# Seven products for the second up-projection pair, its block sums made during the attention

## The chip, the cores and the metric

The kernel runs on one core of a Trainium2 chip. TensorE does the matrix products, VectorE and ScalarE the elementwise work, GpSimd (POOL) a few scalings and the issue of accumulating transfers, SyncE the issue of the other transfers. The metric is device time in microseconds (us) of one execution. Every time below is in us unless ns is written.

## The reference

One layer of a decoder: forgetting attention, a residual with layer norm, a gated MLP with a causal depthwise convolution, another residual with layer norm, and a gated embedding. 512 rows, width 1024, all in float32. The part that the change touches is the MLP's first product:

```python
def conv_ffn(x, w_up, conv_w, conv_b, w_down):
    u, g = jnp.split(x @ w_up, [FFN_DIM], axis=-1)      # x 512 x 1024, w_up 1024 x 5632
    g = causal_dwconv(g, conv_w, conv_b)                # three taps along the rows
    return (jax.nn.gelu(g, approximate=False) * u) @ w_down   # w_down 2816 x 1024
...
x = layer_norm(ALPHA * x + fox_mixer(x, ...), ...)
x = layer_norm(ALPHA * x + conv_ffn(x, ...), ...)
gate = sigmoid(x @ ple_w_gate + ple_b_gate)
x = x + gate * (p @ ple_w_proj)
```

## The kernel before

**Numbers in two parts.** Each float32 operand is split into a high part (rounded to the matmul's format) and a low part, and each product is three matmuls: high x high, high x low, low x high (`three`, its matmul is L159). A weight piece is cut in two steps: ScalarE copies it to `whi` (L130), VectorE subtracts to make `wlo` (L136). With `by_dma` the low part is made in another way: ScalarE writes the negated high part into `wlo` (L132), and POOL issues a transfer that adds the weight onto it from DRAM (L133).

**The weight stream.** The class `Weights` holds a list of pieces ("units") of 128 x 1024 float32 in the order of use. `load_to` loads them into four raw buffers; some pieces instead go to a part of a tile called `side`, chosen by `spare` (`W.more`), so that more loads are in flight. `cut_to` cuts them, into five `whi` and five `wlo` buffers. `get(i, 4)` cuts up to piece i+4 before the product on piece i is emitted. Some pieces carry a `make`: VectorE adds or subtracts blocks before the cut (`t12` L215 and L216, `up_t3` L229, `t4` L237).

**The up-projection in pairs.** The 22 column blocks of `w_up` (f) are taken as pairs j = f // 2, numbered from 0, so j = 1 is the second pair. A plain pair is four pieces (u and g of two blocks), each with 8 x 3 matmuls of 512 rows' columns, in `up`. The pairs in `UP_PAIRS` are computed by a Strassen-like scheme with seven half-size products instead of eight (`up_step`): stages 0, 1 and 2 have one piece for g (s = 0) and one for u (s = 1), with 24 matmuls of 256 columns each; stage 3 has one piece for both. After stage 0 ScalarE copies half of the bank away (`side(7)`, L913) and zeroes that half (L914), and VectorE adds the other half to the copy (L918); after stage 1 ScalarE copies both halves out (L922, L923, L925); after stage 2 VectorE subtracts the whole bank (L929); after stage 3 ScalarE copies (L933). The scheme needs sums of the input's blocks (`x_sums`, made once) and sums of weight blocks. Those weight sums come from one of three places:

- pairs in `KEPT`: VectorE makes them during the attention (`keep_load`, `keep_sums`), and they are kept in DRAM;
- pairs in `IN_DRAM`: a copy of the blocks is made in DRAM (`up_copies`, issued at heads in `COPIES`), then accumulating transfers add blocks in DRAM (`sums_beside`, one step at each place in `BESIDE`);
- the others: the `make` functions on the spot.

Each step of `sums_beside` is a one-column ScalarE copy (L320), a one-column POOL copy behind it (L321), and a POOL transfer (L322). After the pairs it also sums blocks of the gate weight.

**The rest of a pair.** The convolution is a ScalarE pass (L855) and two VectorE passes (L856, L858), then Gelu on ScalarE (L863) and the product on VectorE (L864). For pairs in `APART` the sums of the previous pair's result (`operand_sums`, L951 to L954) and its split (`operand_parts`, L959 and L960) are made in this pair's stage 0. The second weight's products (`down`) follow one group of three pairs later, a few between the stages of the pairs from j = 3 on (`between`, `CHUNKS`); pairs 0 to 2 have none between their stages.

**Order.** A planner orders the instructions by estimated times. From the second pair to the end of the MLP's pairs, VectorE and ScalarE are held to the order of the program:

```python
if f == 2:
    ordered.enter_context(tc.manual_schedule(
        engines={mybir.EngineType.DVE, mybir.EngineType.Activation}))
```

After the pairs comes a remainder of the second product (`r`), four times `norm`, then the embedding and the gate (again with block sums, loaded as `gt`).

Of the kernel before, what the change touches and what calls it, by code (L numbers as in the profile page):

```python
# [12 lines left out]
AF = mybir.ActivationFunctionType  # L13
# [3 lines left out]
P = 128  # L17
# [13 lines left out]

CHUNKS = (None,) + ((1,) * 8 + (0, 1, 2, 1),) * 2 + ((1, 1, 2, 1, 2, 2, 2, 1),)

UP_PAIRS = (2, 3, 4, 5, 6, 7, 8, 9)

KEPT = (3, 4, 5, 6, 7)

IN_DRAM = (8,)

BESIDE = {2: (0, 2, 3), 3: (0, 2, 3), 4: (0, 2, 3), 5: (0, 2), 6: (0, 2, 3), 7: (0, 2), 8: (0, 2, 3),  # L40
          9: (0, 2, 3), 10: (0, 2)}

DMA_PAIRS = (1, 2)

APART = (2, 3, 4, 5, 6, 7, 8, 9)
HALF = S // 2
ALPHA = 2.0 ** 0.25
EPS = 1e-5
# [9 lines left out]
RAW_BUFS = 4  # L58

COPIES = (2, 3)  # L60

BANKS = ("six", "six", "two", "six", "six", "six", "two", "six")
SPLIT_BUFS = 5
# [86 lines left out]
def trunk_layer(ctx: ExitStack, tc: tile.TileContext, xT, x2d, pT, w0, wqk, wv1, wv2, bf, wo, wup, cwb,  # L150
                wdn, wpl, wg, bg, gm, bm, gf, bff, out):
    nc = tc.nc
# [21 lines left out]
    W = Weights(tc, base)  # L174
# [78 lines left out]
    def up_units(j):  # L253

        f0, f1 = 2 * j, 2 * j + 1
        if j in KEPT + IN_DRAM:
            return (lambda q: W.add(wup[f0, 1 - q], inner=P),
                    lambda q: W.add(kept[j, q][:, 0:4:3, :], inner=512),
                    lambda q: W.add([(kept[j, q][:, 2, :], 512), (wup[f1, 1 - q][:, 4:], 512)]),
                    lambda q: W.add([(kept[j, i][:, 1, :], 512) for i in range(2)]))  # L260

        def unit(f, q, make=None):
            return W.add(wup[f, 1 - q], inner=P, make=make, by_dma=make is None and j in DMA_PAIRS)

        add = nc.vector.tensor_add
        return (lambda q: unit(f0, q), lambda q: unit(f1, q, t12(wup[f0, 1 - q][:, :4], 3 + q, add)),
                lambda q: unit(f1, q, up_t3),
                lambda q: W.add([(wup[f0, 1 - i][:, 4:], 512) for i in range(2)], make=t4(3, op=add)))

    dram = ctx.enter_context(tc.tile_pool(name="dram", bufs=1, space=bass.MemoryType.DRAM))  # L270
    kept = {(j, q): dram.tile([P, 4, 512], F32, name=f"kept{j}_{q}")
            for j in KEPT + IN_DRAM for q in range(2)}

# [18 lines left out]
    def up_copies():  # L292

        for j in IN_DRAM:
            for q in range(2):
                for n in range(2):
                    nc.sync.dma_start(kept[j, q][:, 2 * n:2 * n + 2, :].rearrange("p a (k b) -> p (a k) b", b=P),
                                      wup[2 * j + n, 1 - q])
                    yield

    def sums_beside():

        def blocks(j):
            for to, src in ((0, None), (2, None), (3, 0), (1, 3)):
                for q in range(2):
                    t = kept[j, q]
                    if src is None:
                        yield (t[:, to, :].rearrange("p (k b) -> p k b", b=P),
                               wup[2 * j + 1, 1 - q][:, 2 * to:2 * to + 4])
                    else:  # L310
                        yield t[:, to, :], t[:, src, :]

        def gates():
            for to, src in (("t1", "b12"), ("t2", "t1"), ("t4", "t2"), ("t3", "b12")):
                for k in range(4):
                    yield quad(to, k, 1), quad(src, k, 1)

        for to, src in itertools.chain(*[blocks(j) for j in IN_DRAM], gates()):
            m = next(steps)
            nc.scalar.activation(small[:, m:m + 1], zeros[:, :1], AF.Copy)  # L320
            with tc.issue_after(nc.gpsimd.tensor_copy(small[:, m + 32:m + 33], small[:, m:m + 1]).ins):  # L321
                nc.gpsimd.dma_start(to, src, accum_op=ALU.add)  # L322
            yield

    u_up, u_dn = {}, [[] for _ in PAIRS]
    for part in range(4):
# [3 lines left out]
        for i in range(2 * len(fs)):  # L330
            f, q = fs[i // 2], i % 2
            j, n = f // 2, i % 4
# [20 lines left out]
    u = u_up[0, 1] + 5  # L353
    while u < len(W.units):
        spare(u, 5)
        both = u_up[2, 3, 0] < u + 3 < u_up[9, 1, 0] - 5
        if both:
            spare(u + 3, 3)
        u += 6 if both else 5
# [20 lines left out]
    zeros = base.tile([P, P], F32, name="zeros")  # L380
# [12 lines left out]
    small = base.tile([P, 96], F32, name="neghalf")  # L393
# [123 lines left out]


    to_keep = [(k, t) for k, t in kept.items() if k[0] in KEPT]
    in_work, made, last_sum, last_mask = [], [], [], []  # L520

    def keep_load(queue=nc.sync):

# [64 lines left out]
    def scores(h):  # L588
        QA, KA, qb, kb = stacks.pop(h)
        pr = ap.tile([P, 10 * P], F32, tag="pr", name=f"pr{h}")  # L590
        nm = ap.tile([P, NT], F32, tag="nm", name=f"nm{h}")
        ls = ap.tile([P, NT], F32, tag="ls", name=f"ls{h}")
        tiles = []
        for i0 in range(0, NT, 2):
            pair = [(bank(f"s{h}_{i}"), slice(i * P, (i + 1) * P), max((i + 1) * P, 256))
                    for i in (i0, i0 + 1)]
            for ps, q, n in pair:
                nc.tensor.matmul(ps[:, :n], QA[:, q], KA[:, :n], start=True, stop=False)  # L598
            for ps, q, n in pair:
                nc.tensor.matmul(ps[:, :n], qb[0:68, q], kb[0:68, :n], start=False, stop=True)  # L600
            tiles += pair
        off = 0
        for i in range(NT):
            w = (i + 1) * P
            ps = tiles[i][0]

            behind = ExitStack()
            if h % 2 and last_sum:
                behind.enter_context(tc.issue_after(last_sum[0]))
            last_mask[:] = [nc.vector.tensor_tensor_reduce(  # L610
                ps[:, :w], ps[:, :w], mask[:, S - w:], -1.0, BIG, op0=ALU.add, op1=ALU.min,
                accum_out=nm[:, i:i + 1]).ins]
            behind.close()
            nc.scalar.activation(pr[:, off:off + w], ps[:, :w], AF.Exp, bias=nm[:, i:i + 1], scale=-1.0,  # L614
                                 accum_out=ls[:, i:i + 1])
            off += w
        rl = ap.tile([P, NT], F32, tag="rl", name=f"rl{h}")
        nc.vector.reciprocal(rl, ls)  # L618
        off = 0
        for i in range(NT):  # L620
            w = (i + 1) * P
            nc.gpsimd.tensor_scalar_mul(pr[:, off:off + w], pr[:, off:off + w], rl[:, i:i + 1])  # L622
            off += w
        probs[h] = pr

# [36 lines left out]
    copies = up_copies()  # L662
# [43 lines left out]
    for h in range(H + 2):  # L706
        m, s = divmod(h, 2)
        if h == 2:
            project(2, 0)
        if h < H:  # L710
            scores(h)
            with tc.issue_after(last_mask[0]):
                for _ in range(2 if h in COPIES else 0):
                    next(copies)

            if s == 0 and h != 2:
                keep_sums()
                keep_load()
        elif s == 0:
            keep_sums()  # L720
            keep_load()
        if m + 1 < KD and h != 2:
            project(m + 1, s)
        for k in OUT_FIRST.get(h, ()):
            out_first(k)
        if s == 1 and h + 1 < H:
            stack(h + 1)
        if 1 <= h < H + 1:
            turn(h - 1)
        if h >= 2:  # L730
            values(h - 2)
        if s == 1 and h + 1 < H:
            stack(h + 2)
        if h == H:
            y = base.tile([P, NT, D], F32, tag="xh", name="y")
            for t in range(NT):
                nc.sync.dma_start(y[:, t, :], x2d[t * P:(t + 1) * P, :])
# [26 lines left out]
    def norm(t, g, b, meanwhile=None):  # L764
        mv = post.tile([P, 4], F32, tag="mv", name="mv", bufs=2)
        nc.vector.bn_aggr(mv[:, 0:2], stats.pop(t))
        nc.vector.tensor_scalar_add(mv[:, 2:3], mv[:, 1:2], EPS)
        nc.gpsimd.tensor_tensor(mv[:, 3:4], mv[:, 2:3], neghalf, op=ALU.pow)
        if meanwhile is not None:
            flip(*meanwhile)  # L770
        nc.vector.scalar_tensor_tensor(y[:, t], y[:, t], mv[:, 0:1], g, op0=ALU.subtract, op1=ALU.mult)
        nc.vector.scalar_tensor_tensor(y[:, t], y[:, t], mv[:, 3:4], b, op0=ALU.mult, op1=ALU.add)

    def flip(t, xh, xl, whole=None):

# [25 lines left out]
    for t in range(NT):  # L801
        a, b = cut_tiles("S", 4, 4, f"x1t{t}", F32)
# [7 lines left out]
    copies = gate_copies()  # L810
# [194 lines left out]
    before = None  # L1005
    pending = []
    beside = sums_beside()
    ordered = ExitStack()
    for part in range(4):
        ops = []  # L1010
# [1 line left out]

        def between():
            if next(place) in BESIDE.get(j, ()):
                next(beside)
            for _ in range(next(slots, 0)):
                next(before)

# [7 lines left out]
        for f in range(6 * part, min(6 * part + 6, NF)):  # L1026
            q, j = f % 2, f // 2
# [95 lines left out]
    for i, t in enumerate(tiles):  # L1123
        tk = slice(t * P, (t + 1) * P)
        for n in range(2):
# [6 lines left out]
                      weights_move=True)  # L1132
            add_half(t, n, ps, False)
            half_stats(t, n)
        norm(t, g2, b2)
        if i == 0:
            W.cut_to(u_pl[1] + 1)
        if i > 1:
# [186 lines left out]
```

## Time and profile before

| | us |
|---|---|
| median of 3 runs | 641.88 |
| lowest, highest | 641.8, 642.21 |
| the profiled execution | 642.98 |
| its span | 641.3 |
| TensorE busy | 635.4 |
| VectorE busy | 545.9 |
| ScalarE busy | 396.8 |
| POOL busy | 135.8 |

In the rows below PE is TensorE, PEld its weight load, DVE VectorE, ACT ScalarE, POOL GpSimd, SP SyncE; a q after the name is the engine's sequencer, which issues transfers and waits. A timeline row is start, duration, engine, line, operation, output<-inputs, shapes, count, and in brackets the idle time ahead of it with what ended it. Starts of neighbours on VectorE are closer than their durations, since one drains while the next begins.

### The profile page before, as it was taken

The page shows a single profiled execution, that of the slowest core. Times are in us where ns is not written, and L with a number is a line of the kernel's source. Part 1 is how long each engine was busy: PE and PEld are TensorE (multiplying, and loading weights), DVE is VectorE, ACT ScalarE, POOL GpSimd, SP SyncE. Part 2 cuts the span into 40 slices and gives each one's busy share as a digit, 9 for nine tenths or more (in the row PEclk, how much of TensorE's full clock was granted, in tenths as well). Part 3 has the DMA queues.
Part 4 walks back from the last instruction along what each step waited for, and adds up shares of the span by engine and source line. Part 5 has one row for each costly group of instructions (what it writes and reads, how often), then busy time and mean ns, then how long its engine had stood idle before and what let it go on. Part 6 is the DMA issues. An engine that isn't in the chain of part 4 may idle for free.

```text
span 641.3 us, 10471 instructions
## 1 busy us (share of the span) xinstructions
PE 635.4 (99%) x3780; PEld 566.2 (88%) x3780; DVE 545.9 (85%) x872; ACT 396.8 (62%) x716; POOL 135.8 (21%) x165
## 2 busy tenths in 40 slices
PE   9999999999999999999999999999999999999997
PEld 7899888888888889989999999999998998888886
DVE  6567779988888699857889989999898999699997
ACT  6264787877876326955766666757565745337772
POOL 2000464554456043110201110010011010002001
PEclk9999999999999999999999999999999999999999
DMA  8896634555678787695885778777769585672632
GB/s 315 279 320 210 225 111 141 189 177 157 205 261 308 262 258 221 142 253 153 209 244 171 206 240 230 229 205 205 218 193 273 155 203 159 180 262 64 228 112 99
DMA packets 54516, 132.66 MB, mean 207 GB/s; under 512 B 5376, under 2 KB 8448, under 8 KB 54464
## 3 DMA queue, kind: packets, MB, share of 16 engines
q1 hardware_dynamic: 48080, 115.60, 54.5%
q0 software_dynamic: 6240, 16.26, 13.3%
q8 instruction: 30, 0.49, 0.3%
q14 instruction: 22, 0.18, 0.1%
q10 hardware_dynamic: 144, 0.13, 0.1%
HBM read 117.16 MB, written 25.17 MB: 222 GB/s over the span
## 4 chain that ended last, share of the span: by engine, by line
PE 92%; DVE 3%; DMA 3%; ACT 1%; issue 1%; DVEq 0%; ACTq 0%; SPq 0%
PE g L159 16%; PE u L159 16%; PE pp L159 14%; PE pv L159 7%; PE x L159 7%; PE pl L159 7%; PE z L159 4%; PE ap L159 3%; PE r L159 3%; PE o L648 3%; PE t L635 2%; PE ao L159 2%; PE y L159 2%; PE s L598 2%; PE s L600 2%; DMA raw<-wdn 1%
## 5 line engine op out<-in xcount | busy, mean ns | idle before, releaser
L130 ACT ACTIVATE whi<-raw 128x1024 fp32r<-128x1024 f32 (+4 forms) x126 | 123.1, 980 | 86.2 <-PE pv L159 18.7
L136 DVE TENSOR_TENSOR wlo<-raw,whi 128x1024 fp32r<-128x1024 f32 (+4 forms) x121 | 134.8, 1121 | 22.3 <-ACT whi L130 22.0
L622 POOL TENSOR_SCALAR pr<-pr,rl 128x128 f32<-128x128 f32 (+1 forms) x64 | 75.7, 1200 | 74.6 <-DVE rl L618 74.6
L321 POOL COPY neghalf<-neghalf 128x1 f32<-128x1 f32 x24 | 9.2, 384 | 244.3 <-ACT neghalf L320 244.3
L159 PE MATMUL pp<-xh,whi 128*128 128x512 f32 (+1 forms) x130 | 50.8, 391 | 0.1
L159 PE MATMUL pp<-xl,whi 128*128 128x512 f32 (+1 forms) x130 | 50.8, 391 | 0.0
L159 PE MATMUL pp<-xh,wlo 128*128 128x512 f32 (+1 forms) x130 | 50.8, 392 | 0.0
L159 PE MATMUL g<-x1h,whi 128*128 128x256 f32 (+1 forms) x160 | 48.9, 306 | 0.8 <-ACT E L933 0.8
L159 PE MATMUL g<-x1l,whi 128*128 128x256 f32 (+1 forms) x160 | 48.7, 304 | 0.0
L159 PE MATMUL g<-x1h,wlo 128*128 128x256 f32 (+1 forms) x160 | 48.7, 304 | 0.0
L159 PE MATMUL u<-x1l,whi 128*128 128x256 f32 (+1 forms) x152 | 47.3, 311 | 0.0
L159 PE MATMUL u<-x1h,wlo 128*128 128x256 f32 (+1 forms) x152 | 47.3, 311 | 0.0
L159 PE MATMUL u<-x1h,whi 128*128 128x256 f32 (+1 forms) x152 | 47.2, 311 | 0.0
L136 DVE TENSOR_TENSOR wlo<-side,whi 128x1024 fp32r<-128x1024 f32 (+1 forms) x39 | 38.8, 1000 | 4.4 <-ACT whi L130 4.4
L130 ACT ACTIVATE whi<-side 128x1024 fp32r<-128x1024 f32 (+1 forms) x40 | 35.1, 883 | 11.1 <-PE u L159 3.4
L614 ACT ACTIVATE pr<-s,nm 128x128 f32<-128x128 f32 (+1 forms) x64 | 33.6, 528 | 11.9 <-DVE nm L610 11.7
L159 PE MATMUL g<-xsh,wlo 128*128 128x256 f32 x128 | 36.2, 283 | 0.0
L159 PE MATMUL u<-xsh,wlo 128*128 128x256 f32 x128 | 36.2, 283 | 0.0
L159 PE MATMUL u<-xsl,whi 128*128 128x256 f32 x128 | 36.2, 283 | 0.0
L159 PE MATMUL u<-xsh,whi 128*128 128x256 f32 x128 | 36.2, 283 | 0.0
L159 PE MATMUL g<-xsl,whi 128*128 128x256 f32 x128 | 36.2, 283 | 0.0
L159 PE MATMUL g<-xsh,whi 128*128 128x256 f32 x128 | 36.1, 282 | 0.0
(638 smaller groups left out, 1958.0 us busy)
## 6 DMA issues: line engine op xcount, KB each, us to landing
raw<-wup SPq DMA_DIRECT2D x27, 512.0 KB, 4.3
raw<-wdn SPq DMA_DIRECT2D x25, 512.0 KB, 4.8
raw<-wqk SPq DMA_DIRECT2D x14, 512.0 KB, 4.4
ka<-wup SPq DMA_DIRECT2D x10, 512.0 KB
kb<-wup SPq DMA_DIRECT2D x10, 512.0 KB, 3.5
kept<-kb SPq DMA_DIRECT2D x9, 512.0 KB, 3.9
kept<-ka SPq DMA_DIRECT2D x9, 512.0 KB
side<-wup SPq DMA_DIRECT2D x9, 512.0 KB, 6.0
```

Of the source, the lines that this page charges most:

```text
L130: self.nc.scalar.activation(hi[:, c:e], piece, AF.Copy)
L136: self.nc.vector.tensor_sub(lo[:, c:e], piece, hi[:, c:e].bitcast(F32))
L159: nc.tensor.matmul(ps, lhsT, rhs, start=start and n == 0, stop=stop and n == 2, skip_group_check=on)
L321: with tc.issue_after(nc.gpsimd.tensor_copy(small[:, m + 32:m + 33], small[:, m:m + 1]).ins):
L598: nc.tensor.matmul(ps[:, :n], QA[:, q], KA[:, :n], start=True, stop=False)
L600: nc.tensor.matmul(ps[:, :n], qb[0:68, q], kb[0:68, :n], start=False, stop=True)
L614: nc.scalar.activation(pr[:, off:off + w], ps[:, :w], AF.Exp, bias=nm[:, i:i + 1], scale=-1.0, accum_out=ls[:, i:i + 1])
L622: nc.gpsimd.tensor_scalar_mul(pr[:, off:off + w], pr[:, off:off + w], rl[:, i:i + 1])
L635: nc.tensor.transpose(ps[:, w:w + P], pr[:, o:o + P], ident)
L648: nc.tensor.matmul(ps[:, q0:], V[:, j, h], p[:, o:o + w], start=j == 0 and n == 0, stop=j == NT - 1 and n == 1)
```

## The change

- `UP_PAIRS` gains j = 1: the second pair runs as seven products. It enters `APART`, and its weight sums are made in the attention (`KEPT`), in the place of j = 7.
- j = 7 goes to `IN_DRAM` with j = 8: four more copies of 512 KB in DRAM, and eight more accumulating transfers. The copies for j = 7 go out on SyncE at heads 2 and 3, as those for j = 8 did; those for j = 8 go out on POOL, one each at heads 5, 7, 9 and 11, behind the head's last scaling.
- `sums_beside` then has 32 steps where it had 24. `BESIDE` still holds 24 of them, from j = 3 on; the last eight are sent two by two after the four last norms, with the norm's result as the input of the one-column copy.
- `DMA_PAIRS` loses j = 2: the third pair's two plain pieces get their low parts from VectorE. Of the second pair the two stage-0 pieces keep theirs by transfer.
- The places at which `side` slots serve as load buffers (`spare`) begin and end a little differently around pairs 2 and 9, and go on after pair 9.

```diff
-UP_PAIRS = (2, 3, 4, 5, 6, 7, 8, 9)
-KEPT = (3, 4, 5, 6, 7)
-IN_DRAM = (8,)
-BESIDE = {2: (0, 2, 3), 3: (0, 2, 3), 4: (0, 2, 3), 5: (0, 2), 6: (0, 2, 3), 7: (0, 2), 8: (0, 2, 3),
-          9: (0, 2, 3), 10: (0, 2)}
-DMA_PAIRS = (1, 2)
-APART = (2, 3, 4, 5, 6, 7, 8, 9)
+UP_PAIRS = (1, 2, 3, 4, 5, 6, 7, 8, 9)
+KEPT = (1, 3, 4, 5, 6)
+IN_DRAM = (7, 8)
+BESIDE = {3: (0, 2, 3), 4: (0, 1, 2, 3), 5: (0, 2, 3), 6: (0, 2, 3), 7: (0, 2, 3), 8: (0, 2, 3), 9: (0, 2, 3), 10: (0, 2)}
+DMA_PAIRS = (1,)
+APART = (1, 2, 3, 4, 5, 6, 7, 8, 9)
+COPIES_LATE = (5, 7, 9, 11)
...
-            return (lambda q: W.add(wup[f0, 1 - q], inner=P),
+            return (lambda q: W.add(wup[f0, 1 - q], inner=P, by_dma=j in DMA_PAIRS),
...
-                    nc.sync.dma_start(kept[j, q][:, 2 * n:2 * n + 2, :].rearrange("p a (k b) -> p (a k) b", b=P),
-                                      wup[2 * j + n, 1 - q])
+                    queue = nc.sync if j == IN_DRAM[0] else nc.gpsimd
+                    queue.dma_start(kept[j, q][:, 2 * n:2 * n + 2, :].rearrange("p a (k b) -> p (a k) b", b=P),
+                                    wup[2 * j + n, 1 - q])
...
+        seen = yield
         for to, src in itertools.chain(*[blocks(j) for j in IN_DRAM], gates()):
             m = next(steps)
-            nc.scalar.activation(small[:, m:m + 1], zeros[:, :1], AF.Copy)
+            nc.scalar.activation(small[:, m:m + 1], zeros[:, :1] if seen is None else seen, AF.Copy)
...
-            yield
+            seen = yield
...
-        both = u_up[2, 3, 0] < u + 3 < u_up[9, 1, 0] - 5
+        both = u_up[2, 3, 0] + 6 < u + 3 < u_up[9, 1, 0] - 6 or u + 3 > u_up[9, 3, 0] + 6
...
+            if h in COPIES_LATE:
+                with tc.issue_after(last_scale[0]):
                     next(copies)
...
-        norm(t, g2, b2)
+        seen = norm(t, g2, b2)
+        for _ in range(2):
+            beside.send(seen)
```

More of the change, by code (lines that the diff above doesn't have):

```diff
@@ L519, in trunk_layer @@
     to_keep = [(k, t) for k, t in kept.items() if k[0] in KEPT]
-    in_work, made, last_sum, last_mask = [], [], [], []
+    in_work, made, last_sum, last_mask, last_scale = [], [], [], [], []
     def keep_load(queue=nc.sync):
@@ L621, in scores @@
             w = (i + 1) * P
-            nc.gpsimd.tensor_scalar_mul(pr[:, off:off + w], pr[:, off:off + w], rl[:, i:i + 1])
+            last_scale[:] = [nc.gpsimd.tensor_scalar_mul(pr[:, off:off + w], pr[:, off:off + w],
+                                                         rl[:, i:i + 1]).ins]
             off += w
@@ L714, in trunk_layer @@
                     next(copies)
+            if h in COPIES_LATE:
+                with tc.issue_after(last_scale[0]):
+                    next(copies)
             if s == 0 and h != 2:
@@ L772, in norm @@
         nc.vector.scalar_tensor_tensor(y[:, t], y[:, t], mv[:, 3:4], b, op0=ALU.mult, op1=ALU.add)
+        return mv[:, 3:4]
     def flip(t, xh, xl, whole=None):
@@ L1007, in trunk_layer @@
     beside = sums_beside()
+    next(beside)
     ordered = ExitStack()
@@ L1014, in between @@
             if next(place) in BESIDE.get(j, ()):
-                next(beside)
+                beside.send(None)
             for _ in range(next(slots, 0)):
```

## The prediction

> Times are microseconds. The profiled execution took 642.98 (span 641.3, the rest lies around it); the median of the three runs shown is 641.88, so 1.1 is taken off any sum made on the profile. From no change, this kernel's measurement can tell 0.2%, about 1.3: faster is below 640.6 here, slower above 643.16.
>
> **What bounds the kernel now.** I read the busy times first, then the chain of work that ended last, then VectorE's timeline where the change falls.
>
> ```profile
> PE 635.4 (99%) x3780; PEld 566.2 (88%) x3780; DVE 545.9 (85%) x872; ACT 396.8 (62%) x716; POOL 135.8 (21%) x165
> ```
>
> TensorE never rests, so a removed matmul counts in full as long as nothing makes TensorE wait. The chain through the second and third pair (window 270.5 to 301):
>
> ```profile
> 270.56 5.44 PE g L159 x24
> ...
> 286.88 5.44 PE u L159 x24
> 292.32 2.87 PE g L159 x24
> 295.19 2.88 PE u L159 x24
> 298.07 2.88 PE g L159 x24
> 300.95 0.12 PE u L159
> ```
>
> Four plain pieces of the second pair, 24 matmuls of 512 columns each, run to 292.32; then the third pair takes 2.88 for 24 matmuls of 256. The windows view of those two stages and of the one ahead of them; its columns are the length, then the busy time of TensorE, its weight load, VectorE, ScalarE and POOL, each with a count, then clock, DMA share and GB/s:
>
> ```profile
> 270.56:292.32 21.76, 21.76 (x98) 18.02 (x98) 13.49 (x21) 11.39 (x17) 2.57 (x3) 1.00 0.84 217
> 292.32:312.47 20.15, 20.15 (x170) 20.15 (x170) 17.08 (x23) 14.17 (x26) 3.15 (x6) 1.00 0.71 194
> 260.00:270.56 10.56, 10.56 (x68) 9.60 (x67) 8.14 (x11) 10.53 (x13) 1.74 (x2) 1.00 0.51 114
> ```
>
> VectorE is busy 13.49 of 21.76 in the second pair and 17.08 of 20.15 in the third: room in the one, little in the other. What it does there, in program order (both engines are held to it from the second pair on):
>
> ```profile
> 287.73 0.75 DVE L856 SCALAR_TENSOR_TENSOR a<-g,cw,a 128x511 f32<-128x511 f32 x1 [2.97 <-ACT a L855]
> 288.51 0.75 DVE L858 SCALAR_TENSOR_TENSOR a<-g,cw,a 128x510 f32<-128x510 f32 x1
> 289.18 0.68 DVE L229 TENSOR_TENSOR raw<-raw 128x512 f32<-128x512 f32 x1
> ...
> 292.43 0.69 DVE L864 TENSOR_TENSOR E<-a,u 128x512 f32<-128x512 f32 x1 [1.36 <-PE u L159]
> 293.03 0.68 DVE L229 TENSOR_TENSOR raw<-raw 128x512 f32<-128x512 f32 x1
> ...
> 296.06 0.42 DVE L918 TENSOR_TENSOR side<-g,side 128x256 f32<-128x256 f32 x1 [1.21 <-ACT g L914]
> 296.41 1.21 DVE L237 TENSOR_TENSOR raw<-raw,side 128x1024 f32<-128x1024 f32 x1
> 297.54 1.22 DVE L136 TENSOR_TENSOR wlo<-raw,whi 128x1024 fp32r<-128x1024 f32 x1
> 298.68 0.42 DVE L951 TENSOR_TENSOR E<-E 128x256 f32<-128x256 f32 x1
> ...
> 300.14 0.42 DVE L918 TENSOR_TENSOR side<-u,side 128x256 f32<-128x256 f32 x1
> 300.47 0.68 DVE L960 TENSOR_TENSOR a1l<-E,a1h 128x512 fp32r<-128x512 f32 x1
> ...
> 304.66 1.23 DVE L136 TENSOR_TENSOR wlo<-raw,whi 128x1024 fp32r<-128x1024 f32 x1 [0.90 <-ACT whi L130]
> ```
>
> The two L918 rows are the ones to watch: each reads the bank in which TensorE goes on accumulating in the next stage, so TensorE cannot enter that stage before it. The second ends at 300.56 and TensorE's next stage begins at 300.95 by the chain: 0.4 of slack, in the kernel before.
>
> **The change part by part.**
>
> *Matmuls.* Plain: 4 x 5.44 = 21.76. Seven products: 168 matmuls of 256 columns, seven pieces of 2.88 = 20.16. TensorE saves 1.60, if never kept waiting. Rows give 227 ns a matmul of 512 and 120 of 256. (The Trainium skill, TensorE: Matmul & The Clock Gate, section Back-to-back issue gap, gives N/2.4 + 2.5 ns; by it the saving would be an estimated 2.4, but the rows decide.)
>
> *VectorE's work.* It gains the lows of five second-pair pieces and of two third-pair pieces (1.22 each), two adds (0.42) and two subtractions of 128x512 (0.68): 8.54 + 0.84 + 1.36 = 10.74. It had 13.49 + 17.08 = 30.57; together 41.3, against 40.3 of TensorE time for both pairs. Two of the lows (2.4) fit ahead of the pair, where VectorE idles 2.4 (8.14 of 10.56). So VectorE is full, and its order decides. I number weight pieces as they are loaded: 4 to 10 second pair, 11 to 17 third; when product n is emitted, piece n+4 is cut. Spacing from start to start in the rows: a cut of 1024 takes 1.14 (297.54 to 298.68); 512 columns 0.60 (292.43 to 293.03), so a cut in two halves 1.20; convolution 1.45 (287.73 to 289.18); block sum of 1024 1.13 (296.41 to 297.54); operand sums 1.46 (298.68 to 300.14). Two more spacings, from VectorE's rows further on, are the block sums of a 1-2 unit (1.33, 325.93 to 327.26) and the way from the second convolution step over Gelu to the product (1.50):
>
> ```profile
> 314.42 0.75 DVE L858 SCALAR_TENSOR_TENSOR a<-E,cw,a 128x510 f32<-128x510 f32 x1
> 315.92 0.69 DVE L864 TENSOR_TENSOR E<-a,E 128x512 f32<-128x512 f32 x1 [0.76 <-ACT a L863]
> ```
> ```profile
> 325.93 0.69 DVE L215 TENSOR_TENSOR raw<-raw,side 128x512 f32<-128x512 f32 x1
> ...
> 327.26 1.82 DVE L136 TENSOR_TENSOR wlo<-raw,whi 128x1024 fp32r<-128x1024 f32 x2
> ```
>
> From the cut of 11 to the third pair's first L918, in program order: cut 11 1.14; sums for 13 1.33, cut 12 1.14; subtraction 0.60; sums for 14 1.33, cut 13 1.20; subtraction 0.60; convolution 1.45; sum for 15 0.60, cut 14 1.20; product 0.60; convolution and Gelu 0.78 + 1.50; product 0.60; sum for 16 0.60, cut 15 1.14. Together 15.81. From there to the second L918 the rows above show 4.08 (296.06 to 300.14), and the same instructions stand there after.
>
> Where the chain begins: the cut of 11 follows ScalarE's three copies of the second pair's stage 1. In the third pair the same place is 300.95 to 304.66, 3.71 after TensorE's end, because those copies wait for VectorE's last operand part:
>
> ```profile
> 302.72 0.39 ACT L922 ACTIVATE E<-g 128x256 f32<-128x256 f32 x1 [0.46 <-DVE s1l L960]
> ```
>
> Without that wait it would be 304.66 - 302.72 = 1.94. The same wait stands in the second pair, with one block sum fewer ahead of it; I take 3.4, nearest to 3.71. Counted from the second pair's start, stage 1's first half ends at 3 x 2.88 = 8.64, cut 11 starts at 12.0, the first L918 at 27.85, the second at 31.93, ended at 32.35. TensorE, never waiting, would enter that stage at 20.16 + 3 x 2.88 = 28.80. It waits 3.55 in all: about 0.7 at the second pair's last stage (the subtraction, done at 19.5, needed at 18.7), then in front of the third pair's stage 1, 1.6 and 1.2. Ends for this term: 2.1 (start 1.94) to 3.9 (3.71). If TensorE needed only the half bank that L918 reads, the 12 matmuls on the other half (1.44) would run ahead and 2.1 would be left. Rows speak for the whole bank: ScalarE's copy of the first half, idle before, starts at the end of both halves.
>
> ```profile
> 295.23 0.38 ACT L913 ACTIVATE side<-g 128x256 f32<-128x256 f32 x1 [2.04 <-PE g L159]
> ```
>
> By the Trainium skill (PSUM — Partial Sum Buffer, section PSUM bank collisions raise a hardware error), two engines must be kept apart by bank, not address; this trace agrees with that at 295.23, and the rule speaks against the change.
>
> In later pairs products of the layer's second weight stand between the stages and give VectorE time; nothing more is lost there.
>
> *Lows by transfer.* Second pair two instead of four, third pair none instead of two. Each costs ScalarE a second pass over the piece, so it gains time. They took:
>
> ```profile
> wlo<-wup POOLq DMA_DIRECT2D x6, 512.0 KB, 8.9
> ```
>
> A piece is cut about 11 ahead of use at 2.88 a piece, so transfers would barely do for pieces 11 and 12; VectorE's lows never come late that way, but they are 2.3 of the chain above.
>
> *Attention.* Five pairs are still summed there, so that load is unchanged. Four DRAM copies more go out on POOL's queue, each behind a head's last scaling, with the next head's scaling queued behind it:
>
> ```profile
> L622 POOL TENSOR_SCALAR pr<-pr,rl 128x128 f32<-128x128 f32 (+3 forms) x27 | 32.0, 1201 | 33.7 <-DVE rl L618 33.7
> ```
>
> POOL idles 33.7 of 60 there, an issue is some 0.8 (next rows), so nothing: bounds 0 to 0.8.
>
> *Sums beside.* Same number per pair; eight accumulating steps move behind the four last norms: each a one-column ScalarE copy that waits for the norm's power, a POOL copy, a POOL issue of 0.8. Queued behind are ScalarE's cuts and the next power on POOL, and SyncE's loads of the third gate sum:
>
> ```profile
> L322 POOL DMA_DIRECT2D gt<-gt x8 | 6.5, 813 | 0.9 <-issue 0.7
> ```
> ```profile
> gt<-gt POOLq DMA_DIRECT2D x8, 256.0 KB, 7.0
> ```
> ```profile
> 591.65 1.46 POOL L768 TENSOR_TENSOR mv<-mv,neghalf 128x1 f32<-128x1 f32 x1 [5.24 <-DVE mv L767]
> ```
> ```profile
> 590.64 0.32 SPq L100 DMA_DIRECT2D morel<-gt  x1
> 593.91 0.32 SPq L100 DMA_DIRECT2D raw<-gt  x1
> ```
>
> The last norm's power ends at 593.1, and with two copies, two issues of 0.8 and 7.0 to land its sums arrive near 602, 11 after the load issued at 590.64. What that load brings is wanted only by the gate's last products, but the one issued at 593.91 stands behind it on SyncE and would move to 602 if the order holds. A planner sets the order there, and may move the load back instead. I take 0; bounds 0 to 2.
>
> *Side slots.* One piece more is preloaded after the ninth pair, and the shift of three pieces moves which ones sit in side slots. The only stall of the middle is at 490.7:
>
> ```profile
> 490.00:500.00 10.00, 9.16 (x66) 8.47 (x65) 8.78 (x14) 6.21 (x13) 0.66 (x2) 1.00 0.69 226
> ```
> ```profile
> 481.61 8.73 DMA raw<-wdn
> ...
> 490.44 1.06 ACT whi L130
> ```
>
> That piece's raw buffer still comes free from the same piece as before, so I keep the stall (0); bounds -1.0 to +1.
>
> **Sum.** -1.60 + 3.55 = +1.95: 644.9 on the profile, 643.8 as a median.
>
> **Rivals.**
> Faster: VectorE keeps up. Decides when the second L918 ends by 28.8 after the pair's start, against my 32.35; the seven cuts must then partly run earlier or the start be near 1.94. For it: VectorE is full in many later stretches, and TensorE does not wait there:
>
> ```profile
> 350.00:360.00 10.00, 10.00 (x75) 9.51 (x74) 9.93 (x17) 7.05 (x12) 0.99 (x2) 1.00 0.69 186
> ```
>
> Against: those have other products in between. Full gain 640.3, with the stall of 490 gone 639.3.
> Same: TensorE waits for the half bank only (2.1 lost, 642.4), or the stall at 490 goes as well (642.8).
> Worse: as forecast and the late gate sums hold up SyncE, ScalarE or VectorE in the tail, +1 to 2: 645 to 646.
> The skill's gap formula: TensorE alone would give an estimated 639.5; the rows leave that 1 in 100.
>
> **How the numbers follow.** Forecast as such 0.50; with a tail 0.08; same-rivals 0.24; VectorE keeps up 0.18. Faster 0.18, same 0.25 (a little of the forecast's edge falls in it), slower 0.57. The forecast's own range is 642.4 to 644.2, from 2.1 to 3.9. For 8 in 10 I reach down to 640.2 and up to 645.3.
>
> **What would show it.** After: VectorE near 20 of 20 busy in the second and third pair; TensorE's pieces of 2.88 from 270.56, gaps just ahead of the third pair's g<-xsh and u<-xsh, released by VectorE's L918; the fourth pair begins at about 314.4 (312.47 before). It is wrong if the third pair shows no gap and the fourth begins at 310.9, if gaps stand in the attention (copies), or if the tail from 562 lasts over 0.5 longer or shorter.

## The result and the profile after

| | before | after |
|---|---|---|
| median of 6 runs each | 641.84 | 649.92 |
| lowest, highest | 641.32, 642.21 | 649.15, 656.33 |
| ratio of after to before, 95% interval | | 1.0143 [1.0104, 1.0181] |
| the profiled execution | 642.98 | 650.83 |
| its span | 641.26 | 649.12 |

The changed kernel is slower: 1.4% by the ratio, which is one of means and holds the one execution of 656.33; 1.3% or 8.1 by the medians; 7.86 by the spans of the two profiled executions. The forecast of 643.8 had the direction; the time lies far above its range. I mark four points of the same work in both traces (us from the span's start):

| first matmul of | before | after | difference |
|---|---|---|---|
| the first pair (g) | 246.71 | 246.63 | -0.08 |
| the fourth pair (g) | 312.31 | 314.29 | +1.98 |
| the remainder (r) | 562.55 | 563.70 | +1.15 |
| the embedding (p) | 602.80 | 603.92 | +1.12 |
| end of the span | 641.26 | 649.12 | +7.86 |

So 2 is lost up to the fourth pair, 0.8 comes back in the middle, and 6.7 is lost behind the start of p, where the diff moves only small things. Busy times of the changed kernel:

```profile
PE 637.3 (98%) x3852; PEld 569.0 (88%) x3852; DVE 555.3 (86%) x883; ACT 400.5 (62%) x735; POOL 146.4 (23%) x181
```

TensorE has 72 matmuls more (168 of half the length in the place of 96) and is busy 1.9 longer, although the change takes 1.6 of its work away: some matmuls must have become slower. What TensorE waited for (total, times, longest):

```profile
PE pl L159 <- ACT moreh L1201: 2.3, 1, 2.3
PE g L159 <- DVE side L925: 2.0, 1, 2.0
PE u L159 <- DVE side L925: 0.9, 1, 0.9
...
PE pl L159 <- DVE sg1h L1204: 0.5, 1, 0.5
PE pl L159 <- DVE wlo L136: 0.4, 1, 0.4
```

The second and third rows are the forecast's (L925 here is the L918 of the kernel before); the three on `pl` are new. The pairs first, in windows (length, then busy time of TensorE, weight load, VectorE, ScalarE, POOL with counts, clock, DMA share, GB/s):

```profile
270.31:290.47 20.16, 20.15 (x167) 19.94 (x166) 16.89 (x26) 13.64 (x24) 0.00 (x0) 1.00 0.58 198
290.47:314.29 23.82, 20.93 (x172) 20.52 (x171) 21.36 (x30) 15.82 (x27) 0.00 (x0) 1.00 0.53 175
...
490.00:500.00 10.00, 10.00 (x75) 9.51 (x74) 9.14 (x13) 5.11 (x10) 0.00 (x0) 1.00 0.85 282
```

The first row is the 20.16 that the second pair was to take instead of 21.76, and TensorE is busy in all of it. (Five matmuls of the third pair run in it; the second pair's last twelve stand behind them, from 289.80 to 291.33.) The second row, up to the fourth pair, takes 23.82 where the third pair took 20.15 before. The last row has no stall: that of 1.0 at 490.7 is gone. Three rows of VectorE's timeline carry the chain of the prediction: the cut of piece 11, then the two sums that free the banks.

```profile
282.32 1.23 DVE L136 TENSOR_TENSOR wlo<-side,whi 128x1024 fp32r<-128x1024 f32 x1 [0.90 <-ACT whi L130]
...
298.14 0.41 DVE L925 TENSOR_TENSOR side<-g,side 128x256 f32<-128x256 f32 x1
...
302.21 0.41 DVE L925 TENSOR_TENSOR side<-u,side 128x256 f32<-128x256 f32 x1
```

And the tail: the chain that ended last, from the last norm on.

```profile
592.80 1.47 POOL mv L774
594.29 0.21 ACT neghalf L322
594.56 0.46 POOL neghalf L323
595.02 0.79 POOL gt L324
595.81 0.26 POOL neghalf L323
596.16 7.50 DMA gt<-wg
603.79 0.32 SPq L100
...
605.16 8.05 DMA raw<-gt
613.24 1.06 ACT whi L130
614.30 0.95 ACT moreh L1201
615.28 1.24 DVE sg1h L1204
616.56 27.72 PE pl L159 x125
```

In the kernel before TensorE alone is on the chain from the first r to 636.6. Here the chain leaves it at 562.5 and runs through VectorE's norms; then come the last norm's power, the one-column copy behind it, POOL's second issue, 7.50 until that accumulating transfer lands, then SyncE's queue, then a load of 8.05, then ScalarE and VectorE. SyncE's queue in that stretch (window 590 to 612):

```profile
SPq L100 <- DMA gt<-wg: 21.3, 2, 15.7
```

Twice it stood still for an accumulating transfer, 15.7 and 5.6 long: the planner had put the loads of the third gate sum between those of the first and the second, as in the kernel before, but now their data came late. When the last sum landed at 603.7, six loads of 512 KB went out in 2.5: the one that had waited and five behind it.

### The profile page after: what moved, and what is told of

Same layout as the page of the kernel before. It is cut to its first block, busy times and chain, and to the rows that moved or that the text cites. A ratio compares the mean times of both kernels' runs of the same rounds, so it can differ in the third digit from the quotient of the medians.

```text
span 649.1 us, 10666 instructions
## 1 busy us (share of the span) xinstructions
PE 637.3 (98%) x3852; PEld 569.0 (88%) x3852; DVE 555.3 (86%) x883; ACT 400.5 (62%) x735; POOL 146.4 (23%) x181
## 4 chain that ended last, share of the span: by engine, by line
PE 86%; DVE 7%; DMA 3%; ACT 1%; issue 1%; POOL 0%; SPq 0%; DVEq 0%; POOLq 0%; ACTq 0%
PE u L159 16%; PE g L159 16%; PE pp L159 13%; PE x L159 7%; PE pv L159 7%; PE pl L159 4%; PE z L159 4%; PE ap L159 3%; PE ao L159 3%; PE o L651 3%; PE t L638 3%; PE y L159 2%; PE s L600 2%; PE s L602 2%; DVE wlo L136 1%; DMA raw<-gt 1%
## 5 line engine op out<-in xcount | busy, mean ns | idle before, releaser
L136 DVE TENSOR_TENSOR wlo<-raw,whi 128x1024 fp32r<-128x1024 f32 (+4 forms) x125 | 140.2, 1128 | 22.0 <-ACT whi L130 21.4
L323 POOL COPY neghalf<-neghalf 128x1 f32<-128x1 f32 x32 | 16.4, 513 | 262.4 <-ACT neghalf L322 262.4
L159 PE MATMUL g<-x1h,wlo 128*128 128x256 f32 (+1 forms) x156 | 45.8, 294 | 0.0
L136 DVE TENSOR_TENSOR wlo<-side,whi 128x1024 fp32r<-128x1024 f32 (+1 forms) x42 | 41.8, 1002 | 3.9 <-ACT whi L130 3.9
L159 PE MATMUL g<-xsh,whi 128*128 128x256 f32 x144 | 40.8, 283 | 2.0 <-DVE side L925 2.0
L159 PE MATMUL u<-xsh,whi 128*128 128x256 f32 x144 | 40.9, 284 | 0.9 <-DVE side L925 0.9
L159 PE MATMUL u<-xsl,whi 128*128 128x256 f32 x144 | 40.8, 283 | 0.0
L159 PE MATMUL u<-xsh,wlo 128*128 128x256 f32 x144 | 40.8, 283 | 0.0
L159 PE MATMUL g<-xsl,whi 128*128 128x256 f32 x144 | 40.8, 283 | 0.0
L159 PE MATMUL g<-xsh,wlo 128*128 128x256 f32 x144 | 40.7, 283 | 0.0
```

The source lines that it names most:

```text
L136: self.nc.vector.tensor_sub(lo[:, c:e], piece, hi[:, c:e].bitcast(F32))
L159: nc.tensor.matmul(ps, lhsT, rhs, start=start and n == 0, stop=stop and n == 2, skip_group_check=on)
```

## The experiments

Theory of the pairs (P): VectorE, in program order and nearly full from the cut of piece 11 to the second L925 (19.38 of 20.31), reaches the two L925 late; its block sums for the third pair are what is too much. Theory of the tail (T): SyncE's queue, held by a load that waits for the late sums of the gate weight; the loads behind it come late and together. Rival to T: the late steps cost something by themselves, on ScalarE, POOL or DMA. Experiments 1 to 4, 5 to 8 and 9 to 12 each ran beside the kernel before on one chip (its medians there: 642.25, 642.56, 642.53). One trace says little about differences under 1: in the four traces of the kernel before and its variants (2, 8 and 11), whose edits lie further on, the first pair begins anywhere from 245.66 to 246.71.

**1. Gate sums back among the pairs.**

```diff
-BESIDE = {3: (0, 2, 3), 4: (0, 1, 2, 3), 5: (0, 2, 3), ...
+BESIDE = {j: (0, 1, 2, 3) for j in range(3, 11)}
...
-        for _ in range(2):
-            beside.send(seen)
```

> The changed kernel with all 32 steps of the sums beside the products inside the pairs (four each for j = 3 to 10), none behind the last norms. Theory (late gate sums hold SyncE, and behind it the loads of t2): the tail goes back to the length it had before, from the first r matmul to the end 78.7 as before instead of 85.4, so about 643.2. Rival (the tail is lost to something else in the change, such as the loads from side slots or buffers shifted by three pieces): it stays near 650. Second rival: eight transfers more in the pairs slow the weight loads there and give back 1 or more, 644 to 646.

Measured 645.0, ratio 1.0041 [1.0027, 1.0054]. From the first r to the end 78.83, where the kernel before has 78.71 and the changed one 85.42: the late sums were the whole of the tail. The median is 1.8 above the 643.2 that I expected, and inside the range of the second rival (eight transfers more among the pairs). The trace shows 0.55 of that from the fourth pair to r (249.96 against 249.41 in the changed kernel), so the rival may have a part. From the second pair's start to the fourth's it is only 0.3 (44.29 against 43.98), although half clock follows the wait: the changed kernel waits 1.09 for the second L925 in that place. The rest lies between executions and chips (the profiled one took 644.33). The stretch of the wait and the one behind it:

```profile
295.32:298.73 3.41, 1.45 (x12) 1.25 (x12) 3.41 (x5) 3.35 (x7) 0.00 (x0) 1.00 0.12 22
298.73:302.14 3.41, 3.41 (x18) 3.41 (x18) 3.38 (x8) 1.00 (x3) 0.00 (x0) 0.50 0.76 233
```

**2. The kernel before, with its last eight gate sums behind the norms.**

```diff
-BESIDE = {2: (0, 2, 3), 3: (0, 2, 3), 4: (0, 2, 3), 5: (0, 2), 6: (0, 2, 3), 7: (0, 2), ...
+BESIDE = {2: (0, 2, 3), 3: (0, 2, 3), 4: (0, 2), 6: (0, 2), 7: (0, 2), 8: (0, 2), 9: (0, 2)}
...
+        for _ in range(2):
+            beside.send(seen)
```

> The kernel before with one part of the change alone: the last eight gate sums (t4, t3) are sent two by two behind the four last norms, with the norm's result as the input of the one-column copy; eight steps fewer in the pairs. Theory (late gate sums): the tail loses 5 to 7 as in the changed kernel, so 646 to 648, about 1 less if the stall at 490 goes with the transfers taken away. Rival (the tail needs another part of the change): within 1 of 641.8.

Measured 646.59, ratio 1.0065 [1.0048, 1.0083]: this part alone makes the kernel before slower, its tail 4.5 longer (83.17). One stretch with TensorE idle, one at half clock:

```profile
609.18:612.59 3.41, 1.37 (x5) 0.56 (x3) 0.87 (x1) 2.90 (x4) 0.00 (x0) 1.00 0.82 297
612.59:616.00 3.41, 3.00 (x7) 2.42 (x8) 3.41 (x6) 3.40 (x5) 0.00 (x0) 0.50 0.05 20
```

**3. The loads of the third and fourth gate sum on POOL's queue instead of SyncE's.**

> The changed kernel, with the four loads of t3 and t4 issued on POOL's queue instead of SyncE's; the sums stay as late as they are. Theory (SyncE is held at the load of t3, the loads of t2 stand behind it): the loads of t2 go out near 602 as before, and most of the 6.7 in the tail comes back, 643 to 645. Rival (the data of t3 and t4 themselves come too late, or the copies behind the norms hold ScalarE and VectorE): it stays within 2 of 650.

A miss: 650.9, ratio 1.0127 [1.011, 1.0143], the tail 86.79. The hold moved to POOL: a load of `gt`, waiting for a buffer, was placed ahead of the last norm's power. POOL's rows there:

```profile
591.28 0.82 POOL L324 DMA_DIRECT2D gt<-wg  x1
598.90 0.59 POOL L100 DMA_DIRECT2D moreh<-gt  x1 [6.80 <-PE pl L159]
599.50 0.58 POOL L775 TENSOR_TENSOR mv<-mv,neghalf 128x1 f32<-128x1 f32 x1
```

It says nothing against T; it shows a second queue on which the same thing happens.

**4. The changed kernel without the third pair's block sums** (that part of the computation is left out).

```diff
-        add = nc.vector.tensor_add
+        add = nc.vector.tensor_add if j > 2 else lambda *a: None
...
-                lambda q: unit(f1, q, up_t3),
+                lambda q: unit(f1, q, up_t3 if j > 2 else lambda t: None if t is None else [t]),
```

> The changed kernel with the third pair's weight block sums left out (five operations on VectorE, 2.66 + 1.20 + 1.13 by the prediction's rows); the tail is left as it is. Theory (VectorE's program order holds up TensorE by 3.4 in front of the third pair's stage 1): the waits at 296 and 301 go, the fourth pair begins near 310.9 instead of 314.3, and the run is 3 to 3.5 shorter than the changed kernel, about 646.5. Rival (TensorE waits there for a load or for ScalarE): the waits stay, and it is within 1 of the changed kernel.

Measured 647.73, ratio 1.0085 [1.0068, 1.0101]; the span is 645.83, 3.3 under the changed kernel's; by the medians it is 5.5 above the kernel before, where the changed kernel is 8.1. Of the two waits on L925 one row of 0.3 is left; the tail is as in the changed kernel.

```profile
PE pl L159 <- ACT moreh L1201: 2.2, 1, 2.2
...
PE g L159 <- DVE side L925: 0.3, 1, 0.3
```

**5. The changed kernel, with the loads of the third and fourth gate sum kept behind the second's on SyncE.** The sums stay behind the norms.

```diff
+    W.behind = {u: u_g["t2"][1] for u in u_g["t3"] + u_g["t4"]}
...
+                    if self.loaded in self.behind:
+                        held.enter_context(self.tc.issue_after(self.issued[self.behind[self.loaded]]))
```

> The changed kernel; the sums of t3 and t4 stay behind the last norms, but their four loads are queued on SyncE behind the loads of t2. Theory (the load of t3's sums holds SyncE at 597 to 603.7 with the loads of t2 behind it): t2 goes out near 602.5, TensorE's 4.9 of waiting at 611 to 616 and the half clock behind it go, the tail is 79 to 80 long from the first r matmul (85.4 in the changed kernel, 78.7 before), the run 643 to 645. Rival (the one-column copies behind the norms, on ScalarE and POOL, cost the time, or t3 itself is too late): the tail stays over 82.

Measured 644.77, ratio 1.0045 [1.0031, 1.006]: 2.2 above the kernel before beside it, where the changed kernel was 8.1 above. So 5.9 of the 8.1 come back from the order of a few loads; the tail is 78.83, and in it TensorE waits for nothing.

```profile
610.00:615.00 5.00, 5.00 (x24) 4.14 (x23) 5.00 (x7) 4.51 (x6) 0.00 (x0) 1.00 1.03 383
```

The DMA share at 610 to 615 is 1.03, as high as in the changed kernel (0.97): crowding does no harm when what is wanted first is issued first. So what costs the time is late data together with this order: it goes when the sums come early (1) and when the loads are ordered (5). It is not the number of late transfers, nor their work on ScalarE or POOL.

**6. As 1, with the third pair's block sums on POOL.**

> All 32 steps in the pairs (as in the run with the gate sums in the pairs), and the third pair's block sums (five operations, 5.0 of VectorE's chain) made by POOL. Theory (VectorE's program order): the waits in front of the third pair's stage 1 shrink from 3.4 to under 0.6 and no half clock follows; 1.6 of matmuls are saved, so 639.5 to 641, below before. Rival (POOL is too slow for it, or its reads slow VectorE): a wait for POOL stands in the same place, 643 or more.

A miss, and the rival's case: 651.4, ratio 1.0145 [1.0132, 1.0159]. While POOL adds, VectorE's subtractions of two operands take from twice to almost four times as long. This kernel, POOL adding 1.44 at 276.76, 1.35 at 278.28, 1.74 at 279.58, 1.33 at 281.40:

```profile
278.41 0.41 DVE L925 TENSOR_TENSOR side<-u,side 128x256 f32<-128x256 f32 x1
278.74 1.43 DVE L967 TENSOR_TENSOR a0l<-E,a0h 128x512 fp32r<-128x512 f32 x1
280.10 1.51 DVE L967 TENSOR_TENSOR b0l<-E,b0h 128x256 fp32r<-128x256 f32 x1
281.53 2.29 DVE L967 TENSOR_TENSOR s0l<-E,s0h 128x1024 fp32r<-128x1024 f32 x1
```

The same three subtractions in experiment 1, where POOL is idle:

```profile
277.38 0.68 DVE L967 TENSOR_TENSOR a0l<-E,a0h 128x512 fp32r<-128x512 f32 x1
277.98 0.41 DVE L967 TENSOR_TENSOR b0l<-E,b0h 128x256 fp32r<-128x256 f32 x1
278.31 1.22 DVE L967 TENSOR_TENSOR s0l<-E,s0h 128x1024 fp32r<-128x1024 f32 x1
```

Their durations add up to 5.23 instead of 2.31: 2.9 more, where the four additions of that stretch take VectorE 2 x 1.33 by the spacing in the prediction. The Trainium skill (GPSIMD Engine Reference, section 1. Specifications) says that POOL's memory interfaces are shared with VectorE, with contention where VectorE's instruction has two such inputs; the rows agree. They show its size too: each of the three ends about its own usual length after the POOL addition beside it (0.54, 0.29 and 1.09 after, for 0.68, 0.41 and 1.22), as if it waited for the whole of that addition. The first row, with one input in the matmul's bank, keeps its 0.41 beside an addition.

This is one half of the miss. Up to the fourth pair the kernel takes 3.6 more than experiment 1 (47.87 against 44.29). Another 3.3 are lost between the fourth pair and r (253.21 against 249.96): at 498.66 TensorE comes out of a wait of 2.3 for a copy that stands behind ScalarE's cut of a `wdn` piece, whose load took 10.20, and runs at half clock after it. Why that load was late here is not shown.

**7. As 1, with the third pair's two plain pieces' lows by transfer again** (`DMA_PAIRS = (1, 2)`).

> All 32 steps in the pairs, and the third pair's two plain pieces get their low parts by transfer again, as before the change. Theory (VectorE's order): its chain is 2.3 shorter, ScalarE's 1.9 longer; the lows of the third pair's first two pieces are issued near 283 and 286 and land 9 to 10 later, 292 to 296, just as or after TensorE wants them (290.7 and 293.6), so TensorE waits there instead, 1 to 3 in all, within 1 of the run with the lows on VectorE (645.0). Rival (transfers land in time): the waits fall to 1.2 or less, 642 to 643.

Measured 644.32, ratio 1.0033 [1.0016, 1.005], within 1 of experiment 1. The waits on L925 are gone, and TensorE waits for the transferred lows instead: 2.3 of VectorE's chain against a transfer that lands late.

```profile
PE u L159 <- DMA wlo<-wup: 2.0, 1, 2.0
PE g L159 <- DMA wlo<-wup: 0.3, 1, 0.3
```

**8. The kernel before, with the new choice of side slots only** (the line `both = ...` of the diff).

> The kernel before with only the new condition for the side slots. Theory A (the new slots take away the stall of 1.0 at 490): 640.9, and TensorE full at 490 to 500. Theory B (that stall hangs on the transfers near it, as in the run of the kernel before with eight steps fewer, where it was gone): the stall stays, within 0.5 of before.

In its trace TensorE does not stall at 490 (10.00 of 10.00 busy from 490 to 500), and its span is 639.4, 1.8 under that of before's profile; 1.05 of this lies ahead of the first pair, 0.8 between it and r. Its time is 642.14, ratio 1.0001 [0.9987, 1.0015]. Inconclusive: the trace shows the stall's end, the times show no gain. Whether the kernel before has that stall in every execution I cannot say; its shortest span on that chip was 639.4 too.

**9 and 10. As 5, with the third pair's sums made in the attention, and another pair's on the spot:** the seventh's (9) or the sixth's (10).

```diff
-KEPT = (1, 3, 4, 5, 6)
+KEPT = (1, 2, 3, 4, 5)
```

(In 10 `KEPT = (1, 2, 3, 4, 6)`; in both the side slots are left free around the pair that makes its own sums.)

> The changed kernel with the third gate sum's and fourth gate sum's loads kept behind the second's (as in e5), and the block sums of the third pair made in the attention in place of the seventh's (KEPT 1 to 5 in place of 1, 3 to 6); the seventh pair makes its own. VectorE's work is the same in all; 5.3 of it (four sums of 1.33 or 1.13) moves from the two pairs without other products between their stages to one that has them. Theory A (VectorE was short of time in the second and third pair only): the 3.2 of waits near 290 to 302 shrink to about 0.5, nothing new stands at the seventh pair, the remainder of the second product begins at 560 to 560.7 (563.2 in e5), the tail keeps 78.8, span 639 to 639.5, median 640 to 641.2, a ratio of 0.996 to 0.998 to the kernel before. Theory B (VectorE is as full in the later pairs, 9.1 to 9.97 of 10 busy by the windows of e5): the waits move to the seventh pair, 2 to 5 in all, half clock after one over 2; median 643 to 646.

Measured 643.9, ratio 1.0022 [1.0013, 1.0031]: the best version with seven products in the second pair that leaves nothing out, still above the kernel before. One wait of 0.3 stays at the third pair, and 1.7 appear at 414.8 and 446.6, in the sixth and seventh pair:

```profile
PE u L162 <- DVE side L929: 1.7, 2, 1.1
...
PE g L162 <- DVE side L929: 0.3, 1, 0.3
```

(L929 is the line that the changed kernel has as L925.) So mostly theory B: of the 3.2 of waits about 0.4 stays, 2.3 moved with the sums (from the fourth pair to r 251.68, in the changed kernel 249.41), and the time is 0.9 under that of 5.

> As e9, but the sixth pair (j = 5) makes its own sums in place of the seventh. It is the last of its group; the windows of e5 show VectorE busy 7.68 of 10 at 370 to 380, just ahead of where its convolution ends, and 9.97 after it. Theory A: as e9, median 640 to 641.2. Theory B: waits of 2 to 5 at 385 to 410, median 643 to 646.

Measured 649.62, ratio 1.0113 [1.0098, 1.0128], worse than either theory. ScalarE's cut of a `wdn` piece is on the chain, behind a load of 9.61, and the copy that TensorE waits for stands behind that cut:

```profile
395.10 9.61 DMA raw<-wdn
...
404.82 0.07 ACT whi L133
...
405.78 0.38 ACT E L944
```

TensorE idles 3.5 from 402.6, then runs at half clock. The same kind of stall returns at 498 (1.5). Why this load was late with the sixth pair and not with the seventh is not settled.

**11. The kernel before, with the late gate sums of 2 and the order of 5.**

> The kernel before with the last eight gate sums behind the norms (as e2) and the loads of the third and fourth gate sum kept behind those of the second (as e5). Theory (the order on SyncE alone costs the tail, and fewer accumulating transfers among the pairs take away the stall of 1.0 at 490): the remainder begins at 561.3 as in e2, the tail falls back from 83.2 to 78.7 to 78.9, span 640.1, median 640.8 to 641.6, ratio 0.997 to 0.9995. Rival (the late sums cost something in the tail whatever the order): tail 80 or more, ratio above 1.001.

Measured 642.19, ratio 0.9997 [0.9988, 1.0006]; r begins at 560.88, the tail is 78.72 (83.17 in 2). T again, on the kernel before. The span is 639.6, 1.7 under that of before's profile (0.8 of it ahead of the first pair), and again the median shows no gain.

**12. Experiments 4 and 5 together** (again with part of the computation left out).

> e4 and e5 together: the changed kernel without the third pair's sums of weight blocks (that part of the computation is left out) and with the loads of the third and fourth gate sum behind those of the second. If the two causes are all that separates the change from its gain: remainder at about 560 (560.1 in e4), tail 78.8, span 639, median 640 to 641, ratio 0.996 to 0.998. If something else is lost too, the ratio stays above 1.000.

Measured 641.85, ratio 0.9998 [0.9988, 1.0008]. Both causes taken out, the 1.4% are gone; but nothing is gained either, and the 0.996 to 0.998 that I expected is not reached. From the second pair's start to the fourth pair's it takes 41.08 (270.23 to 311.31); before, 41.91. So of the 1.6 only 0.8 is left even then: one wait of 0.42 at 296 stays, and 0.3 to 0.4 in smaller pieces. The tail is 79.36, 0.5 longer than in 5; why is open.

## Why the prediction was right in direction and wrong in size

**The pairs: right to a tenth.** By the prediction the cut of 11 starts 12.0 after the second pair's start, the first L918 15.81 later, and TensorE enters stage 1's second half 32.35 after the start. The trace has 282.32 - 270.31 = 12.01, 298.14 - 282.32 = 15.82, and 302.68 - 270.31 = 32.37. The fourth pair begins at 314.29, forecast 314.4. The chain's length was worked out; its start was in part luck, since 3.4 was chosen between 1.94 and 3.71 (3.37 measured). The split into three waits was off (0.7, 1.6, 1.2 forecast; 0.17, 2.12, 1.09 measured): TensorE ran five matmuls of the third pair, 0.6, in the first wait, and waited about as much longer in the second, whose end VectorE sets. One sign did not come: VectorE is busy 16.89 of the second pair's 20.16, not near 20. Up to the cut of 11 it is busy 8.85 of 12.01 and waits for ScalarE in between; only from there on is it nearly full (19.38 of 20.31). The half-bank rival and the rival that VectorE keeps up both fall by this, and experiment 4 shows the cause: without the sums the waits go.

**The side slots: I kept the stall (0); the trace shows it gone (-1.0).** That was one of the bounds. It is gone in experiment 8 with the new slots alone and in 11 without them, so what ended it is not shown, nor what it is worth as a median.

**The attention: right.** The first pair begins 0.08 earlier; the copies cost nothing there that shows beside the spread of 1.05 between traces.

**The tail: the step that failed.** Under *Sums beside* the prediction wrote that the load issued at 593.91 "stands behind it on SyncE and would move to 602 if the order holds", and then "I take 0; bounds 0 to 2". The mechanism was named and it happened: experiments 1, 5 and 11 show it by undoing the late sums and by changing only the order. (The load named went out at 597.76; the loads that were hit are the second sum's, further back in the queue.) But the term measures 6.7, not 0, and even its upper bound was a third of that; the forecast's own sign of being wrong, a tail over 0.5 longer, came. One rival was this case in kind ("Worse", the late gate sums holding up SyncE or ScalarE, +1 to 2), with a chance of 0.08 and a price a third of what it took. Three things were missing in it:

- *The hold came with more behind it.* I looked at one load behind the wait; five more went out with the one that had waited. Released together, they share the DMA engines: the first load of the second sum took 8.05 to land. In the kernel before, the row of SyncE's queue and the row of DMA issues for the same loads are:

```profile
602.49 1.45 SPq L100 DMA_DIRECT2D raw<-gt  x2
...
raw<-gt SPq DMA_DIRECT2D x2, 512.0 KB, 4.0
```

Counted from the first r, this load was issued 1.5 later than before (605.16 - 563.70 against 602.49 - 562.55) and took 4.05 longer to land. The crowding weighs more than the hold.

- *ScalarE's order.* Its cut waits 5.8 for that load (2.7 before), and the copy that makes the gate's next input stands behind the cut. The cut in the changed kernel, then in the kernel before:

```profile
613.24 1.06 ACT L130 ACTIVATE whi<-raw 128x1024 fp32r<-128x1024 f32 x1 [5.77 <-DMA raw<-gt]
...
606.49 1.06 ACT L130 ACTIVATE whi<-raw 128x1024 fp32r<-128x1024 f32 x1 [2.71 <-DMA raw<-gt]
```

I took the third sum's loads as wanted "only by the gate's last products", and asked when their data were needed, not what stood behind them in each queue.
- *The clock.* After the waits TensorE ran at half clock for 6.83:

```profile
611.25:614.66 3.41, 1.38 (x5) 0.67 (x4) 0.48 (x1) 1.42 (x2) 0.00 (x0) 1.00 1.01 378
614.66:621.49 6.83, 5.73 (x13) 4.16 (x14) 6.21 (x8) 6.79 (x9) 0.00 (x0) 0.50 0.22 78
```

A matmul of 512 columns then takes 0.43 instead of 0.23; eleven of them make 2.2 of the 6.7, the waits and their surroundings the other 4.5. Nothing in the prediction has a price for a wait beyond its own length.

**The sum.** By the four marks: -0.1 (up to the first pair) - 1.6 (TensorE) + 3.7 (waits in the pairs) - 0.8 (the middle, the stall in it) + 6.7 (tail) = +7.9, the 7.86 measured. The forecast had -1.6 and +3.55 in it and 0 for the rest.

## What to carry to other kernels

When work is moved later, list for each in-order queue what stands behind the first instruction that waits for it, and price the release too: what was held goes out at once and competes. A term whose mechanism you can name should be priced by what is queued behind it, not taken at 0 because a planner might avoid it. And where two engines are nearly full, cutting work on the one buys only what the other's program order leaves: here 0.8 of 1.6 with every other cause removed.

## What the runs showed of the hardware

**A wait of 2 can cost half clock for 3.4.** The granted clock changes in stretches of 3.41. In the fourteen traces every such stretch at full clock with TensorE busy for 1.51 or less was followed by one at half clock (the tail above and experiments 1, 2, 3, 4, 6, 7 and 10), and none with 1.9 or more was. A second one at half clock followed where TensorE was busy for 2.95 or less of the first (the tail above, 4 and 10), and full clock where it was busy for 3.00 or more. In the changed kernel's pairs the same wait of 2.12 fell across the border of two stretches, and the clock stayed full:

```profile
293.83:297.25 3.42, 2.82 (x24) 2.62 (x22) 2.63 (x5) 2.09 (x4) 0.00 (x0) 1.00 0.39 144
297.25:300.66 3.41, 2.05 (x17) 2.05 (x18) 3.41 (x4) 2.64 (x6) 0.00 (x0) 1.00 0.41 132
```

So the limit lies between 1.5 and 1.9 of idle time in one stretch here. The Trainium skill (TensorE: Matmul & The Clock Gate, section What's actually happening) gives a free-running window of 3413 ns, and the stretches agree; its section Why this matters for your kernels warns of idle gaps over some 3 us, and here 2 in one stretch is enough.

**POOL's additions hold up VectorE's instructions with two inputs outside the matmul's banks** (experiment 6): three that take 2.31 alone took 5.23.
